# A rebuilt head and a rebuilt output norm in a hybrid decoder layer

## The chip, the cores and the metric

The kernel runs on one core of a Trainium2 chip. The metric is device time in microseconds (us) of one execution. The core has a TensorE (PE, with its weight loads as PEld), a VectorE (DVE), a ScalarE (ACT), a GpSimd (POOL) and a SyncE (SP), which here only issues DMAs.

## The reference, cut to what matters

One layer, one sequence of 512 tokens, width 2048, all in float32. The change touches the first norm with its modulation and the last norm.

```python
c_act = jax.nn.silu(c)
mod = c_act @ ada_w + ada_b                 # 2048 x 6144
shift, scale, gate = mod[:D], mod[D:2 * D], mod[2 * D:]
h = rms_norm(x, pre_gain) * (1.0 + scale) + shift
proj = h @ w_in                             # 2048 x 12416 columns
...                                         # RWKV-7 mixer, short convolution, their gates
m = sigmoid(g_a) * y_a + sigmoid(g_b) * y_b
o = m @ w_out
x = x + gate * rms_norm(o, post_gain)       # rms_norm(v, g) = v * rsqrt(mean(v*v) + 1e-6) * g
```

## The kernel before, in words

Everything up to the output product is transposed: channels lie on the 128 partitions, the 512 tokens along the free axis. x is 16 tiles `xT[k]` of 128 x 512, k over the channels. A product in float32 is made of three matmuls of rounded halves (`three`, lines 160 to 162): each operand is split into an upper half (`H`, by ACT) and the remainder (`L`, by POOL or DVE; `split`, lines 148 and 149).

The head (to line 297) has to bring the first tile of h to the PE. Its order is written out by hand for all five engines. SP issues 16 x tiles (line 202), with the two 1 MB pieces of `ada[0]` between the eighth and ninth x and behind the last; then three blocks of input weights (`fraw`, line 215), the two pieces of `ada[1]`, three more blocks, `ada[2]`, one block, `ada[3]`. `ada[j, 0]` holds the transposed columns of the shift for channels of tile j (128 x 2048), `ada[j, 1]` those of the scale. Their product with silu(c) is a reduction along the free axis on DVE (`columns`, line 245, with an accumulated sum); for that silu(c) lies as a row in all partitions in PSUM (`csr`, line 273, PE spreads a one-partition row `crow`). ACT then makes the two per-channel numbers `md` (`scales`, lines 251 and 252).

In the head the sum of squares over the channels is made by PE: ACT squares each x tile (line 268), PE adds them with a weight of ones into `pss` (line 270), turned per four tiles to another group of 32 columns. ACT copies the sums (line 275), PE brings the sums to tokens on partitions (`pst`, line 278), DVE makes the inverse root with integer start and three Newton steps (`rsqrt`, lines 139 to 144), spreads it (`rsb`, line 284), and PE turns it back to tokens along the free axis (`psr`, line 287). The pair `xs` (DVE, line 257), `hH` (ACT, line 259) and `hL` (DVE, line 262) gives the halves of the first h tile.

Behind it stands the joint: the first 16 output tiles of the input product (`fps`), begun while the other tiles of h are still being made, block after block of channels. Its order is computed by a planner in the kernel's text, which keeps a clock `now` and expected landings (`lands`, `come`) from constants, and writes out the order of all engines. Evictions of partial sums go to DVE (line 366) or to ACT and POOL (lines 370 and 371). From there to the end the order is likewise written out or given by Tile, and the PE's main work is `ps_c` (line 1041), the rest of the input product and the mixer beside it.

At the end the output product runs token-major: `o[i][n]` is 128 tokens by 512 columns, i over four rows of tokens, n over four quarters. The first three quarters keep `o` in SBUF, multiplied by `gg` (gate times post gain). For the last quarter the weights stay in SBUF and i is the outer loop: 48 matmuls, then ACT squares and sums (`osum`, line 1268), DVE multiplies by `gg` (line 1300) and makes the inverse root (lines 1301, 139 to 144), ACT and POOL make the first quarter of the output (lines 1303 and 1304), DVE the other three (line 1308), SP sends them (line 1309). For i = 3 nothing follows that could hide this.

Of the kernel before, what the change touches and what calls it, by code (L numbers as in the profile page):

```python
# [8 lines left out]
F32 = mybir.dt.float32  # L9
# [67 lines left out]
def trunk(ctx: ExitStack, tc: tile.TileContext, xT_d, x_d, prm_d, crow_d, ada1_d, ada2_d, rows_d, w_d, lora_d, pa_d, pb_d,  # L77
# [108 lines left out]
    with tc.tile_pool(name="ap", bufs=1) as ap, tc.tile_pool(name="psa", bufs=1, space=PSUM) as psa:  # L186
# [44 lines left out]
        orow = ap.tile([P, P], F32, name="orow")[0:1, :]  # L231
        G.memset(orow, 1.0)
# [3 lines left out]
        cth = ap.tile([P, D], F32, tag="ada", bufs=NADA, name="cth")[0:1, :]  # L236
        A.activation(cth, crow, AF.Tanh, scale=0.5)
        V.scalar_tensor_tensor(crow, cth, 1.0, crow, ALU.add, ALU.mult)
        csr = psa.tile([P, D], F32, name="csr")

        def columns(j, i):
# [3 lines left out]
            V.scalar_tensor_tensor(ada[j, i], ada[j, i], 0.5, csr, ALU.mult, ALU.mult, accum_out=accs[j][:, i:i + 1])  # L245
# [3 lines left out]
        def scales(j):  # L249
            md[j] = ap.tile([P, 2], F32, tag="md", bufs=3, name=f"md{j}")  # L250
            A.activation(md[j][:, 1:2], accs[j][:, 1:2], AF.Identity, bias=ab1[:, j:j + 1], scale=pc("pre", j))
            A.activation(md[j][:, 0:1], accs[j][:, 0:1], AF.Identity, bias=pc("ab", j))
# [12 lines left out]
        pss = bank("mm", "pss")  # L265
        for k in range(KT):
            sq = ap.tile([P, T], F32, tag="t", bufs=3, name=f"sq{k}")
            A.activation(sq, xT[k], AF.Square)
            g = 32 * (k % 4)
            TE.matmul(pss[g:g + 32, :], ones[:, 0:32], sq, start=(k < 4), stop=(k >= KT - 4), tile_position=(0, g))  # L270
# [4 lines left out]
        A.activation(sums, pss, AF.Copy)  # L275
        pst = bank("pg", "pst", 4)
# [1089 lines left out]
```

## Time and profile before

| | |
|---|---|
| median of the three runs shown | 1635.5 us |
| lowest and highest | 1628.7 and 1635.64 us |
| the profiled execution: time, span | 1627.16 us, 1625.1 us |
| its mean granted TensorE clock | 0.994 |
| busy: PE, weight load, DVE, ACT, POOL | 98%, 81%, 57%, 39%, 50% of the span |
| moved by DMA | 235.71 MB, mean 145 GB/s |

The numbers of the trace are from the one profiled execution and counted from its span's start. A row of the timeline has the start, the length, the engine (a q behind it for its queue), the line, the operation, what it writes and reads, and in brackets how long the engine had been idle and what ended that. Differences are to be set against 1627.16 us when they come from its rows, and against the median when runs are compared.

### The profile page before, as it was taken

Reading aid. Unit: us, or ns where it says so; the run is one execution under the profiler, and the core shown is the slowest. Engines: PE = TensorE matmul, PEld = TensorE weight load, DVE = VectorE, ACT = ScalarE, POOL = GpSimd, SP = SyncE. Lnnn points to the kernel's source line nnn. Section 1 sums busy time; section 2 is a strip of 40 time slices with the busy share of each in tenths; the row PEclk is TensorE's granted clock in tenths of the full one; section 3 lists DMA queues with packets and bytes.
Section 4 is the critical chain, followed back from the end, with each engine's and each line's share of the span. In section 5 each row is a group of like instructions: output and inputs, shape, how many; then the busy total and the mean of one; then the engine's idle time right before and its main releaser. Section 6 shows DMA issues by size and latency. Waiting matters only on the chain.

```text
span 1625.1 us, 23142 instructions
## 1 busy us (share of the span) xinstructions
PE 1593.1 (98%) x8152; PEld 1314.3 (81%) x8152; DVE 934.3 (57%) x1660; ACT 639.1 (39%) x1299; POOL 812.8 (50%) x649
## 2 busy tenths in 40 slices
PE   6999999999999999999999999999999999999997
PEld 2788878888888888888888888888888888888885
DVE  4998297863978827826869359353111354463315
ACT  4554352324545235335543353344433223322511
POOL 2699564553445534543535435434354446764421
PEclk8999999999999999999999999999999999999999
DMA  8986334333332342333333433433353886675704
GB/s 315 379 327 236 104 108 122 92 102 105 96 85 85 103 118 83 98 113 111 93 99 97 121 103 93 128 102 115 92 168 119 243 252 202 201 210 166 234 25 156
DMA packets 138885, 235.71 MB, mean 145 GB/s; under 512 B 34833, under 2 KB 43665, under 8 KB 134673
## 3 DMA queue, kind: packets, MB, share of 16 engines
q1 hardware_dynamic: 138624, 234.15, 46.3%
q8 instruction: 64, 1.05, 0.3%
q14 instruction: 51, 0.42, 0.1%
q10 hardware_dynamic: 146, 0.09, 0.0%
HBM read 214.79 MB, written 19.14 MB: 144 GB/s over the span
## 4 chain that ended last, share of the span: by engine, by line
PE 95%; DVE 3%; ACT 1%; issue 0%; DMA 0%; POOL 0%; DVEq 0%; ACTq 0%; POOLq 0%
PE ps_c L1041 53%; PE fps L162 3%; PE fps L161 3%; PE fps L160 3%; PE po L161 3%; PE po L160 3%; PE po L162 3%; PE py_a L162 2%; PE py_b L162 2%; PE py_a L160 2%; PE py_b L161 2%; PE py_b L160 2%; PE py_a L161 2%; PE pg L730 2%; PE pl L162 1%; PE pl L161 1%
## 5 line engine op out<-in xcount | busy, mean ns | idle before, releaser
L428 POOL TENSOR_TENSOR wL_c<-raw_c,wH_c 128x512 fp32r<-128x512 f32 x324 | 441.9, 1365 | 535.9 <-ACT wH_c L428 503.2
L1041 PE MATMUL ps_c<-hH,wL_c 128*128 128x512 f32 x1296 | 513.3, 396 | 0.7 <-POOL wL_c L428 0.7
L1041 PE MATMUL ps_c<-hH,wH_c 128*128 128x512 f32 x1296 | 513.6, 396 | 0.0
L1041 PE MATMUL ps_c<-hL,wH_c 128*128 128x512 f32 x1296 | 512.0, 395 | 0.0
L428 ACT ACTIVATE wH_c<-raw_c 128x512 fp32r<-128x512 f32 x324 | 204.1, 630 | 420.9 <-PE ps_c L1041 265.8
L1041 PEld LDWEIGHTS ps_c<-hH,wL_c 128*128 128x128 f32 x1296 | 243.7, 188 | 48.4 <-POOL wL_c L428 1.1
L1041 PEld LDWEIGHTS ps_c<-hL,wH_c 128*128 128x128 f32 x1296 | 243.8, 188 | 47.2
L1041 PEld LDWEIGHTS ps_c<-hH,wH_c 128*128 128x128 f32 x1296 | 243.8, 188 | 46.9
L149 POOL TENSOR_TENSOR fL<-fraw,fH 128x512 fp32r<-128x512 f32 x56 | 79.0, 1417 | 55.5 <-ACT fH L148 55.3
L428 DVE TENSOR_TENSOR invt<-M,Xg 128x60 f32<-128x60 f32 (+24 forms) x248 | 93.8, 378 | 7.9
L149 POOL TENSOR_TENSOR oL<-wo,oH 128x512 fp32r<-128x512 f32 x48 | 64.7, 1354 | 62.3 <-ACT oH L148 58.8
L160 PE MATMUL fps<-hH,fH 128*128 128x512 f32 x224 | 88.8, 396 | 3.6 <-ACT hH L259 3.6
L428 DVE TENSOR_TENSOR Xg<-Xg,invt 128x60 f32<-128x60 f32 (+24 forms) x248 | 87.2, 352 | 7.9
L161 PE MATMUL fps<-hL,fH 128*128 128x512 f32 x224 | 88.8, 396 | 1.9 <-DVE hL L262 1.9
L162 PE MATMUL fps<-hH,fL 128*128 128x512 f32 x224 | 88.4, 395 | 1.7 <-POOL fL L149 1.7
L428 DVE TENSOR_TENSOR GG<-pg,gmask 128x512 f32<-128x512 f32 x32 | 22.1, 692 | 108.5 <-PE pg L730 108.5
L245 DVE SCALAR_TENSOR_TENSOR ada<-ada,csr 128x2048 f32<-128x2048 f32 x32 | 72.6, 2277 | 10.0 <-PE csr L273 10.0
L161 PE MATMUL po<-oL,mH 128*128 128x512 f32 x192 | 74.9, 390 | 0.0
L160 PE MATMUL po<-oH,mH 128*128 128x512 f32 x192 | 74.7, 389 | 0.0
L162 PE MATMUL po<-oH,mL 128*128 128x512 f32 x192 | 74.7, 389 | 0.0
L148 ACT ACTIVATE oH<-wo 128x512 fp32r<-128x512 f32 x64 | 38.6, 627 | 74.9 <-PE po L162 49.6
L149 POOL TENSOR_TENSOR wL_pb<-raw_pb,wH_pb 128x512 fp32r<-128x512 f32 x32 | 42.5, 1330 | 45.3 <-ACT wH_pb L148 45.3
(268 smaller groups left out, 2584.4 us busy)
## 6 DMA issues: line engine op xcount, KB each, us to landing
raw_c<-in_w_dram SPq DMA_DIRECT2D x324, 256.0 KB, 2.7
ada<-in_ada_dram SPq DMA_DIRECT2D x32, 1024.0 KB, 9.3
gr<-in_ada_dram SPq DMA_DIRECT2D x64, 256.0 KB, 4.4
wo<-in_wo_dram SPq DMA_DIRECT2D x64, 256.0 KB, 3.9
fraw<-in_w_dram SPq DMA_DIRECT2D x56, 256.0 KB, 4.4
raw_pb<-in_pb_dram SPq DMA_DIRECT2D x32, 256.0 KB, 2.7
raw_pa<-in_pa_dram SPq DMA_DIRECT2D x32, 256.0 KB, 2.7
th_s<-th SPq DMA_DIRECT2D x30, 256.0 KB, 2.0
```

Source lines behind the costliest of these rows:

```text
L148: A.activation(H, src, AF.Copy)
L149: eng.tensor_tensor(L, src, H.bitcast(F32), ALU.subtract)
L160: TE.matmul(ps, wH, xH, start=start, stop=False)
L161: TE.matmul(ps, wH, xL, start=False, stop=False)
L162: TE.matmul(ps, wL, xH, start=False, stop=stop)
L245: V.scalar_tensor_tensor(ada[j, i], ada[j, i], 0.5, csr, ALU.mult, ALU.mult, accum_out=accs[j][:, i:i + 1])
L428: f(*args, **kw)
L730: TE.matmul(four(pg)[:, k, :], BK[:, c0 + k, i, :], AR[:, c0 + k, :], start=True, stop=True)
L1041: TE.matmul(ps, w[:, i, :], x[k], start=(k == k0 and x is hH and w is H), stop=(k == KT - 1 and w is L))
```

## The change

In the head, x comes first and without ada pieces between. Four DMAs of 512 KB bring `adan`, the shift's and scale's columns for tile 0 in the layout of the weights (channels of c on partitions). PE multiplies them with silu(c) (16 matmuls in four groups of 32 columns into `psc`, summed over the groups by a further matmul with `every`), so that DVE's two reductions of tile 0 go. ACT still squares x; DVE adds 13 of the squares to the first in SBUF (`acc`), PE sums this and the two left alone (8 and 12) over the channels at once into tokens on partitions. silu(c) as a row in all partitions now comes from `cs` by PE. The root is spread with a PE transpose. The planner's constants are set anew.

At the end the inverse root is a square root on ACT, a reciprocal on DVE and one Newton step. For i = 3 the second quarter is copied to PSUM by ACT, the third stays in PSUM and the fourth is multiplied in place in PSUM; DVE's order is written out for i = 3.

```diff
-        crow = ap.tile([P, D], F32, tag="ada", bufs=NADA, name="crow")[0:1, :]
-        A.dma_start(crow, crow_d)
...
         for k in range(KT):
             S.dma_start(xT[k], xT_d[k])
-            if k == 7:
-                fetch(0, (0,))
-        fetch(0, (1,))
+        adan = [ap.tile([P, KT // 2, 2 * P], F32, tag="ada", bufs=NADA, name=f"adan{i}") for i in range(2)]
+        for i in range(4):
+            q = slice(i % 2 * 4, i % 2 * 4 + 4)
+            S.dma_start(adan[i // 2][:, q, :], adan_d[i // 2, :, q, :])
...
-        orow = ap.tile([P, P], F32, name="orow")[0:1, :]
-        G.memset(orow, 1.0)
...
-        cth = ap.tile([P, D], F32, tag="ada", bufs=NADA, name="cth")[0:1, :]
-        A.activation(cth, crow, AF.Tanh, scale=0.5)
-        V.scalar_tensor_tensor(crow, cth, 1.0, crow, ALU.add, ALU.mult)
+        csb = ap.tile([P, KT, HB], F32, name="csb")
+        V.tensor_copy(csb, cs.unsqueeze(2).to_broadcast([P, KT, HB]))
+        every = ap.tile([P, 1], F32, name="every")
+        V.tensor_reduce(every, ident.rearrange("p (a b) -> p a b", b=HB)[:, :, 0], mybir.AxisListType.X, ALU.add)
+        pcs = bank("pg", "pcs")
+        TE.matmul(pcs[0:KT, 0:P], cs, ident, start=True, stop=True)
+        csT = ap.tile([P, P], F32, name="csT")
         csr = psa.tile([P, D], F32, name="csr")
+        def silu_rows():
+            A.activation(csT[0:KT, :], pcs[0:KT, 0:P], AF.Copy)
+            for k in range(KT):
+                TE.matmul(csr[:, k * P:(k + 1) * P], ident[0:KT, k:k + 1].to_broadcast([KT, P]), csT[0:KT, :], start=True,
+                          stop=True)
...
-        pss = bank("mm", "pss")
+        acc = ap.tile([P, T], F32, name="sqsum")
+        pst = bank("pg", "pst", 12)
+        def by_token(r, sq):
+            for i in range(4):
+                TE.matmul(pst[:, 4 * r + i:4 * r + i + 1], sq[:, i * P:(i + 1) * P], ones[:, 0:1], start=True, stop=True)
+        alone = (8, 12)
         for k in range(KT):
...
             A.activation(sq, xT[k], AF.Square)
-            g = 32 * (k % 4)
-            TE.matmul(pss[g:g + 32, :], ones[:, 0:32], sq, start=(k < 4), stop=(k >= KT - 4), tile_position=(0, g))
-            if k in (4, 6, 8, 10):
-                q = slice((k - 4) // 2 * T, (k - 2) // 2 * T)
-                TE.matmul(csr[:, q], orow, crow[:, q], start=True, stop=True)
-        sums = ap.tile([P, T], F32, tag="t", bufs=3, name="sums")
-        A.activation(sums, pss, AF.Copy)
-        pst = bank("pg", "pst", 4)
-        for i in range(4):
-            TE.matmul(pst[:, i:i + 1], sums[:, i * P:(i + 1) * P], ones[:, 0:1], start=True, stop=True)
-        columns(0, 0)
+            if k == 1:
+                silu_rows()
+            if k in alone:
+                by_token(1 + alone.index(k), sq)
+            elif k:
+                V.tensor_tensor(acc, acc, sq, ALU.add)
+        by_token(0, acc)
+        psc = bank("mm", "psc", 2 * P)
+        for k in range(KT):
+            g = 32 * (k % 4)
+            TE.matmul(psc[g:g + 32, :], csb[:, k, :], adan[k // 8][:, k % 8, :], start=(k < 4), stop=(k >= KT - 4),
+                      tile_position=(0, g))
+        sums = ap.tile([P, 2 * P], F32, name="sums")
+        A.activation(sums, psc, AF.Copy)
+        halve()
...
-            TE.matmul(psr[:, i * P:(i + 1) * P], rsb[:, i, :], ident, start=True, stop=True)
-        columns(0, 1)
-        halve()
-        scales(0)
+            TE.transpose(psr[:, i * P:(i + 1) * P], rsb[:, i, :], ident)
+        pcol = bank("pg", "pcol", 2)
+        for i in range(2):
+            TE.matmul(pcol[:, i:i + 1], sums[:, i * P:(i + 1) * P], every, start=True, stop=True)
+        scales(0, pcol)
...
-        clk = dict(dve=now + 1.4, act=now + 0.7, pool=now + 1.5, dma=now + 15.2)
-        ready, lands, cut = {0: now}, {1: now + 1.0, 2: now + 9.0, 3: now + 15.2}, {b: now + 0.4 * b for b in range(3)}
-        come = {b: now + 1.5 + 0.7 * (b - 3) for b in range(3, 6)}
-        come[6] = now + 9.7
+        clk = dict(dve=now + 1.4, act=now + 0.7, pool=now + 1.5, dma=now + 16.5)
+        ready, lands, cut = {0: now}, {1: now + 2.0, 2: now + 9.8, 3: now + 16.5}, {b: now + 0.4 * b for b in range(3)}
+        come = {b: now + 2.7 + 0.7 * (b - 3) for b in range(3, 6)}
+        come[6] = now + 10.5
...
-                o[i][n] = yslot(f"o{i}_{n}", pool=yc if n < 2 else yp)
+                o[i][n] = pso[i] if (i, n) == (3, NQ - 2) else yslot(f"o{i}_{n}", pool=yc if n < 2 else yp)
...
+            V.tensor_scalar(rs[:, 1:2], rs[:, 0:1], -0.5, None, ALU.mult)
...
+            if i == 3:
+                o1 = bank("pc", "o1")
+                A.activation(o1, o[i][1], AF.Copy)
+                o[i][1] = o1
...
             osum(i, NQ - 1, ps)
-            og = ev.tile([P, T], F32, tag=("u", "cv")[i % 2], bufs=1, name=f"ol{i}")
+            s3, r, y, u, h = ssq[:, i, NQ - 1:NQ], rs[:, 2:3], rs[:, 3:4], rs[:, 4:5], rs[:, 5:6]
+            A.activation(r, s3, AF.Sqrt, scale=1.0 / D, bias=rs[:, 0:1])
+            V.tensor_scalar(h, s3, -0.5 / D, rs[:, 1:2], ALU.mult, ALU.add)
+            og = ps if i == 3 else ev.tile([P, T], F32, tag=("u", "cv")[i % 2], bufs=1, name=f"ol{i}")
             V.tensor_tensor(og, ps, gg[NQ - 1], ALU.mult)
-            V.tensor_scalar(rs[:, 1:2], ssq[:, i, NQ - 1:NQ], rs[:, 0:1], 1.0 / D, ALU.add, ALU.mult)
-            rsqrt(rs[:, 2:3], rs[:, 1:2], rs[:, 3:4])
-            A.activation(o[i][0], o[i][0], AF.Copy, scale=rs[:, 2:3])
+            V.reciprocal(y, r)
+            V.scalar_tensor_tensor(u, y, h, y, ALU.mult, ALU.mult)
+            V.scalar_tensor_tensor(y, u, 1.5, y, ALU.add, ALU.mult)
+            A.activation(o[i][0], o[i][0], AF.Copy, scale=y)
```

More of the change, by code (lines that the diff above doesn't have):

```diff
@@ L244, in columns, with scales @@
                 accs[j] = ap.tile([P, 2], F32, tag="acc", bufs=3, name=f"acc{j}")
-            V.scalar_tensor_tensor(ada[j, i], ada[j, i], 0.5, csr, ALU.mult, ALU.mult, accum_out=accs[j][:, i:i + 1])
+            V.scalar_tensor_tensor(ada[j, i], ada[j, i], 1.0, csr, ALU.mult, ALU.mult, accum_out=accs[j][:, i:i + 1])
         xs, md = {}, {}
-        def scales(j):
+        def scales(j, sums=None):
+            sums = accs[j] if sums is None else sums
             md[j] = ap.tile([P, 2], F32, tag="md", bufs=3, name=f"md{j}")
-            A.activation(md[j][:, 1:2], accs[j][:, 1:2], AF.Identity, bias=ab1[:, j:j + 1], scale=pc("pre", j))
-            A.activation(md[j][:, 0:1], accs[j][:, 0:1], AF.Identity, bias=pc("ab", j))
+            A.activation(md[j][:, 1:2], sums[:, 1:2], AF.Identity, bias=ab1[:, j:j + 1], scale=pc("pre", j))
+            A.activation(md[j][:, 0:1], sums[:, 0:1], AF.Identity, bias=pc("ab", j))
         def modulate(j, rstd):
@@ new lines, in trunk @@
+        alone = (8, 12)
+        for k in range(KT):
+            if k == 0:
+                sq = acc
+            elif k in alone:
+                sq = ap.tile([P, T], F32, tag="s", bufs=3, name=f"sq{k}")
+            else:
+                sq = ap.tile([P, T], F32, tag="t", bufs=3, name=f"sq{k}")
+            A.activation(sq, xT[k], AF.Square)
+            if k == 1:
[4 more added lines that the diff above has]
+                V.tensor_tensor(acc, acc, sq, ALU.add)
@@ L280, in trunk @@
+        by_token(0, acc)
+        psc = bank("mm", "psc", 2 * P)
+        for k in range(KT):
+            g = 32 * (k % 4)
+            TE.matmul(psc[g:g + 32, :], csb[:, k, :], adan[k // 8][:, k % 8, :], start=(k < 4), stop=(k >= KT - 4),
[3 more added lines that the diff above has]
+        halve()
         ms = ap.tile([P, 3, 4], F32, name="ms")
[L281 removed]
+        V.tensor_reduce(ms[:, 0], pst.rearrange("p (r i) -> p i r", i=4), mybir.AxisListType.X, ALU.add)
@@ L282, in trunk @@
+        V.tensor_scalar(ms[:, 0], ms[:, 0], 1.0 / D, RMS_EPS, ALU.mult, ALU.add)
         rsqrt(ms[:, 1], ms[:, 0], ms[:, 2])
@@ L1288, in trunk @@
         for i in range(4):
-            rs = cst.tile([P, 4], F32, tag="rs", bufs=2, name=f"ors{i}")
+            rs = cst.tile([P, 6], F32, tag="rs", bufs=2, name=f"ors{i}")
             V.tensor_reduce(rs[:, 0:1], ssq[:, i, 0:NQ - 1], mybir.AxisListType.X, ALU.add)
-            V.tensor_scalar(rs[:, 0:1], rs[:, 0:1], D * RMS_EPS, None, ALU.add)
+            V.tensor_scalar(rs[:, 0:1], rs[:, 0:1], 1.0 / D, RMS_EPS, ALU.mult, ALU.add)
+            V.tensor_scalar(rs[:, 1:2], rs[:, 0:1], -0.5, None, ALU.mult)
             xr = [mslot(f"xr{i}_{n}") for n in range(NQ)]
@@ L1333, in _lay @@
                                                  lnx_bias, conv_w)], axis=1),
-        "crow": np.asarray(c).reshape(1, D),
+        "adan": np.concatenate([ada[:, 0:P], ada[:, D:D + P]], 1).reshape(2, KT // 2, P, 2 * P).transpose(0, 2, 1, 3),
         "ada1": ada[:, :2 * D].reshape(D, 2, KT, P).transpose(2, 1, 3, 0),
```

14 lines of the change are left out of this document (8 added, 6 removed).

## The prediction

> **What bounds the kernel now.** I read the page's head first, then the busy times by stretch, then the order of time in the first 31 us and the last 11, and last the DMA queue's waits. 0.5% of 1635.5 us, about the least that a measurement of this kernel can tell from no change, is 8.2 us.
>
> ```profile
> PE 95%; DVE 3%; ACT 1%; issue 0%; DMA 0%; POOL 0%; DVEq 0%; ACTq 0%; POOLq 0%
> 0.00:31.00 31.00, 17.60 (x57) 5.93 (x57) 12.05 (x29) 15.38 (x26) 4.54 (x18) 0.89 0.86 316
> 31.00:80.00 49.00, 43.93 (x174) 34.37 (x175) 42.33 (x44) 26.71 (x54) 28.18 (x22) 0.93 0.95 370
> 80.00:1614.00 1534.00, 1531.55 (x7924) 1274.04 (x7922) 874.30 (x1573) 595.57 (x1218) 778.42 (x610) 1.00 0.44 135
> 1614.00:1625.10 11.10, 0.00 (x0) 0.00 (x0) 5.63 (x16) 1.41 (x3) 1.68 (x1) 0.68 0.27 94
> ```
>
> The first line is the chain of work that ended last. The four after it are stretches: us, then busy PE, weight load, DVE, ACT and POOL, then granted clock, DMA share, GB/s. From 80 us to 1614 the PE is busy for 1531.55 of 1534 us: a us won ahead of that stretch reaches the end, and so does one won behind it. Three places can move: the head (31 us until the first product matmul), the joint behind it (31 to 80 us, 5.1 us of PE idle, DMA 0.95 busy) and the end (11.1 us without a matmul). The whole head and end are 42 us, 2.6% of the span.
>
> **The head.** In order of time (start, length):
>
> ```profile
> 14.14 1.05 PE L270 MATMUL pss<-sq,ones 128*32 128x512 f32 x4
> 22.22 1.05 PE L278 MATMUL pst<-ones,sums 128*128 128x1 f32 x8 [0.69 <-ACT sums L275]
> 23.31 0.16 DVE L281 TENSOR_SCALAR ms<-pst 128x4 f32<-128x4 f32 x1 [2.71 <-PE pst L278]
> 26.19 0.43 DVE L284 COPY rsb<-ms 128x512 f32<-128x512 f32 x1
> 26.53 2.28 DVE L245 SCALAR_TENSOR_TENSOR ada<-ada,csr 128x2048 f32<-128x2048 f32 x1
> 26.67 2.08 PE L287 MATMUL psr<-ident,rsb 128*128 128x128 f32 x8 [3.40 <-DVE rsb L284]
> 28.86 0.39 ACT L251 ACTIVATE md<-acc,ab,prm 128x1 f32<-128x1 f32 x1 [6.17 <-DVE ada L245]
> 29.27 0.75 DVE L257 SCALAR_TENSOR_TENSOR xs<-x,md,psr 128x512 f32<-128x512 f32 x1 [0.46 <-ACT md L251]
> 30.12 0.72 ACT L259 ACTIVATE hH<-xs,md 128x512 fp32r<-128x512 f32 x1 [0.17 <-DVE xs L257]
> 30.89 0.80 PE L160 MATMUL fps<-hH,fH 128*128 128x512 f32 x1 [2.14 <-ACT hH L259]
> ```
>
> Three steps stand one behind the other: the squares' sums (to 22.2, behind the last x tile), the root on DVE (23.31 to 26.19), and the second ada reduction behind it on DVE (26.53 to 28.8). The scale waits for the last. The change takes both 2.28 us reductions of tile 0 off DVE (two matmul groups take their place) and no longer feeds them through the same megabytes. When do the data land? The issue of the last megabyte of ada tile 0, its us from issue to landing, the pace in that stretch, and the squares as a group:
>
> ```profile
> 12.91 0.33 SPq L199 DMA_DIRECT2D ada<-in_ada_dram  x1
> ada<-in_ada_dram SPq DMA_DIRECT2D x1, 1024.0 KB, 7.3
> DMA packets 157, 0.29 MB, mean 410 GB/s; under 512 B 17, under 2 KB 17, under 8 KB 157
> L268 ACT ACTIVATE sq<-x 128x512 f32<-128x512 f32 x16 | 9.1, 619 | 5.4 <-PE pss L270 5.4
> ```
>
> Issued at 12.91, it lands at 20.2. At 410 GB/s its 1.05 MB take 2.56 us, an x tile 0.64. The last x tile is issued ahead of it, so it has landed at 17.6.
>
> - *x first.* SP issues 16 x tiles and then four adan pieces (512 KB each, 2 MB, as the two ada megabytes before). The last x lands at 17.6 less the other ada megabyte, which now stands between the eighth and the ninth x: 17.6 - 2.56 = 15.0. The last adan piece lands where the last ada did, 20.2. The crow load on ACT's queue goes; it lay beside the others.
> - *Squares by DVE.* ACT's 16 squares stay (0.62 us each, just below the arrival pace); they no longer wait for PE. 13 adds on DVE: no add of two SBUF operands stands in the head, the nearest row is 0.75 us (xs). So: last square 15.6, last add 16.4, four column sums (the x8 row of pst, 1.05) 17.5, reduce and scale 0.4, root 2.9 (23.31 to 26.19) less its 0.2: rsb at 20.6 to 21.1.
> - *Shift and scale by PE.* 16 matmuls of 32 columns by 256; the last four wait for the last adan piece. The pss row has two steps of 512 in 1.05, so 0.26 for one of 256. Ends: 0.5 (four column groups at once) and 1.8 (one after the other). I take four times 0.26, because that row has the same 32 columns: 21.25. Transposes: 2.08 if like psr now, half if they are one pass; I take 1.55: 22.8. Two column sums, half of the pst row: 0.53, so 23.35. The copy of the sums and the first weight split (ACT, 0.6 each) lie beside the transposes.
> - *From there as now*: scale 28.86 to 29.27, xs to 30.12, hH to 30.89: 2.03. First product matmul at 25.4. Ends: 24.7 (rsb at 21.1, one-pass transposes) and 26.7 (1.8 and 2.08). Against 30.9 that is 5.5, between 4.2 and 6.2.
> - *Hidden*: the 16 csr matmuls and the csT copy run while x lands (PE idles there); csb and every (DVE, each at most an rsb, 0.43) ahead of the first add. If that cover went, the csr matmuls would push the column sums, which have 3 us until psc ends. The removed tanh over crow and its product were hidden and bring nothing, nor does POOL's memset of orow. The ada buffers: crow and cth go, adan takes two, so the fetch of tile 2 finds free buffers; it still stands on SP's queue behind three weight loads that wait for the splits of POOL.
>
> **How much of it passes the joint.** SP's queue and the DMA engines in the 14 us around the start (40 slices of 0.35 us from 26), and two later issues:
>
> ```profile
> 17.07 14.62 SPq L215 DMA_DIRECT2D fraw<-in_w_dram  x3
> 31.74 0.93 SPq L199 DMA_DIRECT2D ada<-in_ada_dram  x2
> DMA  8899962100000000001599689999999889988669
> 39.98 0.97 SPq L199 DMA_DIRECT2D ada<-in_ada_dram  x2
> ada<-in_ada_dram SPq DMA_DIRECT2D x1, 1024.0 KB, 11.2
> 52.37 2.27 DVE L245 SCALAR_TENSOR_TENSOR ada<-ada,csr 128x2048 f32<-128x2048 f32 x1
> 59.40 2.28 DVE L245 SCALAR_TENSOR_TENSOR ada<-ada,csr 128x2048 f32<-128x2048 f32 x1
> 61.60 0.75 DVE L262 SCALAR_TENSOR_TENSOR hL<-xs,md,hH 128x512 fp32r<-128x512 f32 x1
> ```
>
> SP stands from 17.07 to 31.7 behind weight loads, and the engines run dry for about 12 slices, 4.2 us. With the splits 5.5 us earlier SP is free at about 26.2, before the engines run dry (28.4): the whole transfer stream behind it moves forward by those 4.2 us, not by 5.5. The slack of the readers takes the rest: the ada megabyte issued at 39.98 lands at 51.2 and is read at 52.37, 1.2 us later. So 4.2 + 1.2 = 5.4 us can pass. The order of the joint is planned anew with landings 0.8 to 1.3 us later after the start; what that does to 5.1 us of PE idle the trace does not show, and I bound it by one DVE reduction either way (2.2 us). I take 5.0 of the 5.5.
>
> **The end.**
>
> ```profile
> 1614.05 0.60 ACT L1268 ACTIVATE osq<-pl 128x512 f32<-128x512 f32 x1 [6.46 <-PE pl L162]
> 1614.77 0.69 DVE L1300 TENSOR_TENSOR ol<-pl,gg 128x512 f32<-128x512 f32 x1 [4.80 <-ACT osq L1268]
> 1615.38 0.20 DVE L1301 TENSOR_SCALAR ors<-ssq,ors 128x1 f32<-128x1 f32 x1
> 1617.74 1.42 DVE L1308 SCALAR_TENSOR_TENSOR xr<-o,ors,xr 128x512 f32<-128x512 f32 x2
> 1618.52 3.13 SPq L1309 DMA_DIRECT2D out_dram<-xr  x4
> 1618.60 1.68 POOL L1304 TENSOR_TENSOR xr<-o,xr 128x512 f32<-128x512 f32 x1 [9.17 <-ACT o L1303]
> 1619.08 1.75 DVE L1308 SCALAR_TENSOR_TENSOR xr<-ol,ors,xr 128x512 f32<-128x512 f32 x1
> 58.52 2.56 POOL L371 TENSOR_TENSOR firsts<-firsts,fs 128x512 f32<-128x512 f32 x2
> 58.79 0.69 DVE L366 TENSOR_TENSOR firsts<-fps,firsts 128x512 f32<-128x512 f32 x1 [0.67 <-PE fps L162]
> ```
>
> From 1615.38 to 1617.74 DVE makes the root: one step of 0.24 and 11 of 0.19. The new one: h (0.2) and the product by gg (0.61 to the next start) on DVE, the square root on ACT beside them, then reciprocal and two steps (3 x 0.19): y at 1614.77 + 0.24 + 0.61 + 0.58 = 1616.2, against 1617.74: 1.5 us. No row has a reciprocal; its ends are the 0.20 and the 0.69 of this fence, and I take 0.19 as for the other one-column steps. The last step on xr takes 1.75 now while POOL runs, 0.75 otherwise. Its operand comes from PSUM in the new kernel, and such a step took 0.69 in the middle of POOL work (last two rows): another 1.0. xr's three steps then end at 1618.2 instead of 1620.8. But y also starts ACT's product and POOL's add: 0.86 after y as now, and 1.28 without a neighbour (half of the two in 2.56), so 1618.4. SP sends the fourth output at 1618.7 and is done at 1619.1 instead of 1621.65: 2.55. The four then follow each other more closely than now, 1 MB in some 2 us, so I take 0.35 off for their own queue: the end gains 2.2 (1.9 to 2.6). In rows 0 to 2 the same edits hide behind the next row's 48 matmuls; the copy of o1 into PSUM (ACT, 0.6) falls into ACT's 6.5 us of idle time before its last square.
>
> **The sum.** 5.0 + 2.2 = 7.2 us. The profiled execution took 1627.16 us (span 1625.1): 1620.0. Its time is 8.3 below the median of the runs shown, which lie between 1628.7 and 1635.64; from the median it is 1628.3.
>
> **Rivals.**
>
> *The clock stays up* (18%). Now the first product matmuls run on half a clock (columns as above):
>
> ```profile
> 22.00:24.00 2.00, 1.05 (x8) 0.97 (x8) 0.65 (x2) 0.69 (x2) 1.17 (x1) 1.00 1.00 416
> 24.00:26.00 2.00, 0.00 (x0) 0.00 (x0) 1.65 (x11) 0.00 (x0) 0.09 (x1) 0.51 1.04 434
> 36.00:37.00 1.00, 1.00 (x4) 0.81 (x3) 0.26 (x2) 0.84 (x3) 0.09 (x1) 0.50 0.99 410
> ```
>
> The clock falls at 24 and is still 0.50 at 36. In the new head PE's pauses before the start are about 1.5 us instead of 3.4 and 2.1. At full clock psc and the transposes would end up to 1.3 us sooner, and the evictions that ACT does before the second scale too: 1.8 us more, 9.0 in all, 1626.5. Against it: PE's work there is thin (one-column and 32-column matmuls). The Trainium skill (TensorE: Matmul & The Clock Gate, Part 1) says that the clock follows activity in a window of about 3.4 us that runs freely; by that rule pauses of 1.5 us could leave it up. The trace agrees in so far as the clock fell after a stretch with little PE work.
>
> *The transfers hold the joint* (17%). The DMA engines are 0.95 busy there; if the stream moves only by its 4.2 us, and weight loads use up the readers' slack, the head passes 3 to 4 and the sum is about 5.5: 1630.
>
> *The square root costs the end its gain* (8%). One table load stands in the trace:
>
> ```profile
> 1.80 1.28 ACT L175 ACT_TABLE_LOAD   x1 [1.80 <-issue]
> ```
>
> If the root needs another table and each row's square takes the first one back, the last row has a 1.28 us load between its sum and its root: r at 1616.3, y at 1616.9, gain of the end 1.5 and of the whole 6.5: 1629. With one load in row 0 alone it is hidden, and that is what I expect. The Trainium skill (ScalarE: Activation LUTs, Table sets: the hidden batching unit) puts sqrt in a set of its own but cheap functions in every set, which makes it one load; with the drain that it adds (2.66 us, What ACT_TABLE_LOAD costs), a load in the last row would leave the end with almost nothing.
>
> *The new order of the joint stalls PE* (7%, the other side). DVE's order is written out: at 59.40 a reduction stands before the lower half hL (61.60) that PE waits for. If the new order puts two reductions (4.4 us) before such a step in two more places, PE loses 8.8: 1635.5 - 7.2 + 8.8 = 1637. At 7.2 us of new idle the gain is gone, at 15.4 the kernel is measurably slower. For it: DVE was busy for 42.33 of those 49 us. Against it: the landings move by 1.3 us at most.
>
> **Chances.** My forecast has 50%. Faster by over 0.5% needs 8.2 us: most of the clock's case, and a good third of the forecast's through its upper ends (6.2 and 2.6) and the spread of the runs: 0.38. Slower: part of the last rival, 0.05. Within: 0.57. The range takes in the lower runs (1628.7 - 9 = 1619.7) and the transfers' case from the highest (1635.6 - 3 = 1632.6), and leaves out the stalled joint.
>
> **What would show it.** First fps matmul at 24.7 to 26.7; no dry stretch of the DMA engines near the start; last x landed near 15; one second table load, near 1575; y about 1.5 us earlier after the last square; the last xr step 0.7 to 0.8; 8.9 us from the last matmul to the end. PE idle between start and 80 us over 7 us, or a start after 27, would make the prediction wrong.

## Result and profile after

The changed kernel takes 1620.38 us (median of five runs, 1618.96 to 1621.57) against 1635.5 us for the kernel before (five runs, 1628.7 to 1636.2): a ratio of 0.9914, 95% interval 0.9894 to 0.9935. The profiled execution took 1618.96 us (span 1617.0) against 1627.16 (span 1625.1), 8.2 us less. Of the 15.1 us between the medians only about 8 can be put down to the change: the times of the kernel before spread over 1626 to 1637 us, and four of its five runs here lie above 1635.

Stretches of the profile after (us, then busy PE, weight load, DVE, ACT, POOL, then granted clock, DMA share, GB/s):

```profile
0.00:31.00 31.00, 23.19 (x110) 18.65 (x111) 19.82 (x44) 16.23 (x29) 6.30 (x18) 0.90 0.97 359
31.00:80.00 49.00, 43.90 (x186) 34.59 (x185) 42.25 (x44) 28.61 (x57) 32.18 (x24) 0.99 0.95 368
80.00:1606.00 1526.00, 1523.61 (x7892) 1268.24 (x7891) 866.00 (x1548) 594.61 (x1216) 772.98 (x606) 1.00 0.45 135
1606.00:1617.00 11.00, 2.32 (x11) 1.59 (x9) 3.33 (x8) 1.70 (x4) 1.26 (x1) 0.79 0.29 95
```

PE's idle time between 31 and 80 us is 5.1 us as before (49 - 43.90), so the joint does not give the head's gain back as idle time. Timeline of the head, PE first and then the other engines around the start (start, length; one row joins the instructions of a line that follow without a pause):

```profile
6.08 7.19 PE L247 MATMUL csr<-csT,ident 16*128 16x128 f32 x32 [0.36 <-ACT csT L245]
13.21 3.57 PE L281 MATMUL pst<-ones,sq 128*128 128x1 f32 x16
16.64 1.85 PE L281 MATMUL pst<-ones,sqsum 128*128 128x1 f32 x8
18.42 3.51 PE L303 MATMUL psc<-adan,csb 128*32 128x256 f32 x32
21.86 0.66 PE L316 MATMUL psr<-ident,rsb 128*128 128x128 f32 x4
22.44 0.61 PE L319 MATMUL pcol<-every,sums 128*128 128x1 f32 x4
25.09 0.79 PE L160 MATMUL fps<-hH,fH 128*128 128x512 f32 x1 [2.04 <-ACT hH L269]
...
21.11 0.43 DVE L313 COPY rsb<-ms 128x512 f32<-128x512 f32 x1
23.09 0.35 ACT L261 ACTIVATE md<-pcol,ab,prm 128x1 f32<-128x1 f32 x1 [0.18 <-PE pcol L319]
28.35 2.29 DVE L254 SCALAR_TENSOR_TENSOR ada<-ada,csr 128x2048 f32<-128x2048 f32 x1
35.16 0.50 PE L160 MATMUL fps<-hH,fH 128*128 128x512 f32 x1 [1.48 <-ACT hH L269]
```

From 6.1 to 23.0 us PE has no pause: no bracket stands in its rows until the first product matmul. So PE's own work ended the head, not a landing: the last `adan` piece had landed at 19.86, the last x tile at 14.7. The first product matmul starts at 25.09 instead of 30.89, 5.80 earlier. The first matmul that needs the second h tile (tile 1) starts at 35.16 instead of 40.90, 5.74 earlier, and the last matmul of the kernel at 1607.93 instead of 1613.57, 5.64 earlier. These two in the kernel before:

```profile
40.90 0.49 PE L160 MATMUL fps<-hH,fH 128*128 128x512 f32 x1 [1.49 <-ACT hH L259]
1613.57 0.39 PE L162 MATMUL pl<-oH,mL 128*128 128x512 f32 x1
```

SP's queue, the DMA engines from 26 to 40 us (40 slices of 0.35 us), and the clock:

```profile
17.29 8.65 SPq L214 DMA_DIRECT2D fraw<-in_w_dram  x3
25.99 1.66 SPq L196 DMA_DIRECT2D ada<-in_ada_dram  x2
DMA  9999999999999989999979999999999999999879
25.00:26.00 1.00, 0.79 (x1) 0.28 (x1) 0.93 (x1) 0.56 (x2) 0.91 (x2) 0.54 0.96 398
28.00:30.00 2.00, 2.00 (x6) 1.59 (x5) 1.95 (x3) 0.63 (x3) 0.00 (x0) 0.50 1.10 408
```

SP is free at 25.99, and the 4.2 us in which the engines ran dry are gone. The clock falls at 25, as it fell before at 24.

The clock column needs care. In the trace the clock's record is a list of entries, each with a start, a length and a share; the column counts time that no entry covers as 1.00. The first entry of this profile stands at 21.67 us: 3.41 us at full clock, then 6.83 us at half from 25.09, then full from 31.91. In the profile before the first entry stands at 10.37: 13.65 us at full clock, then 13.65 us at half from 24.02. What the column shows ahead of a first entry is no measurement, and the pace of the matmuls says that the clock was at half there (shown with the head alone, below).

The end, in order of time:

```profile
1607.93 0.39 PE L162 MATMUL pl<-oH,mL 128*128 128x512 f32 x1
1609.08 0.29 ACT L1341 ACTIVATE ors<-ssq,ors 128x1 f32<-128x1 f32 x1
1609.81 0.15 DVE L1346 RECIPROCAL ors<-ors 128x1 f32<-128x1 f32 x1
1610.44 0.75 DVE L1353 SCALAR_TENSOR_TENSOR xr<-o,ors,xr 128x512 f32<-128x512 f32 x1
1611.22 2.14 SPq L1354 DMA_DIRECT2D out_dram<-xr  x4
1611.30 1.26 POOL L1350 TENSOR_TENSOR xr<-o,xr 128x512 f32<-128x512 f32 x1 [9.17 <-ACT o L1349]
1611.77 0.74 DVE L1353 SCALAR_TENSOR_TENSOR xr<-pl,ors,xr 128x512 f32<-128x512 f32 x1
```

The inverse root is ready 1.36 us after the sum (1609.08 to 1610.44) instead of 2.97 (1614.77 to 1617.74). The last step on `xr` takes 0.74 instead of 1.75 although POOL runs beside it. From the last matmul's end to the span's end it is 8.7 us instead of 11.1.

### The profile page after: what moved, and what is told of

The parts are those of the page before. It is cut to its first block, busy times and chain, and to the rows that moved or that the text cites. A ratio compares the mean times of both kernels' runs of the same rounds, so it can differ in the third digit from the quotient of the medians.

```text
span 1617.0 us, 23221 instructions
## 1 busy us (share of the span) xinstructions
PE 1593.0 (99%) x8194; PEld 1323.1 (82%) x8194; DVE 931.4 (58%) x1643; ACT 641.2 (40%) x1305; POOL 812.7 (50%) x648
## 3 DMA queue, kind: packets, MB, share of 16 engines
q8 instruction: 65, 1.06, 0.3%
## 4 chain that ended last, share of the span: by engine, by line
PE 95%; DVE 3%; ACT 1%; issue 0%; DMA 0%; POOL 0%; POOLq 0%; ACTq 0%
PE ps_c L1071 53%; PE fps L162 3%; PE fps L161 3%; PE fps L160 3%; PE po L161 3%; PE po L160 3%; PE po L162 3%; PE py_a L162 2%; PE py_b L161 2%; PE py_a L160 2%; PE py_b L160 2%; PE py_b L162 2%; PE py_a L161 2%; PE pg L760 2%; PE pl L162 1%; PE pl L161 1%
## 5 line engine op out<-in xcount | busy, mean ns | idle before, releaser
L149 POOL TENSOR_TENSOR fL<-fraw,fH 128x512 fp32r<-128x512 f32 x56 | 79.8, 1434 | 45.6 <-ACT fH L148 45.4
L458 DVE TENSOR_TENSOR Xg<-Xg,invt 128x60 f32<-128x60 f32 (+24 forms) x248 | 92.3, 372 | 7.9
L458 DVE TENSOR_TENSOR invt<-M,Xg 128x60 f32<-128x60 f32 (+24 forms) x248 | 87.1, 351 | 7.9
L254 DVE SCALAR_TENSOR_TENSOR ada<-ada,csr 128x2048 f32<-128x2048 f32 x30 | 68.1, 2275 | 0.0
```

Source lines behind the costliest of these rows:

```text
L149: eng.tensor_tensor(L, src, H.bitcast(F32), ALU.subtract)
L254: V.scalar_tensor_tensor(ada[j, i], ada[j, i], 1.0, csr, ALU.mult, ALU.mult, accum_out=accs[j][:, i:i + 1])
L458: f(*args, **kw)
```

## Experiments

**Head alone, end alone, and before again.** The first has the new head with the old end section, the second the old head with the new end; the third is the kernel before, unchanged, as a measure of what the comparison can tell.

```diff
 e1_head:  head, joint, planner constants of after; end section of before
 e2_end:   head, joint, planner constants of before; end section of after
```

> The new head alone, with the end of the kernel before. Theory (two independent gains): the first product matmul stands at 25.1 us as in the changed kernel, 5.7 us of that reach the last matmul, and the end keeps its 11.1 us: the span of the profile is 1619.4 us. Rival (the runs' larger difference of 15 us comes from the joint): the runs of this kernel alone already lie at 1621 to 1624, some 12 us below those of the kernel before, though the profile's span differs by 5.7.

> The new end alone, with the head of the kernel before. Theory: first product matmul at 30.9, last matmul as before, 8.7 instead of 11.1 us behind it: the profile's span is 2.4 us below that of the kernel before, 1622.7. Rival for the runs' 15 us: the end takes away something that the single profile of the kernel before did not show, and the runs fall by more than 5 us.

> The kernel before once more, to see in a profile where its runs of 1635 us lose 8 us against its profiled execution of 1627. Theory: the time differs from execution to execution in the joint or the head (PE idle between 0 and 80 us); a profile of about 1633 us span would show PE idle there above 5.1 us. Rival: the whole run is slower by the same share, as the pace of the matmuls from 80 us on would show (PE busy 1531.55 of 1534 us now).

Measured against the same 24 runs of the kernel before (median 1629.76): head alone 1623.68 (ratio 0.9946, 0.9926 to 0.9965), end alone 1626.76 (0.9981, 0.9961 to 1.0001), before again 1630.08 (1.0002, 0.9982 to 1.0023). 6.1 and 3.0 us: the parts add up to the whole (9.2 us for the changed kernel with the old planner constants, next experiment, against the same 24 runs). The interval of the end alone just reaches 1, so its gain is read from the profile: the last matmul starts at 1615.08 in a span of 1624.2, 9.1 us before the end against 11.5 (1613.57 to 1625.1), which makes 2.4 us.

Both profiles missed their expected spans, 1621.7 instead of 1619.4 (head alone) and 1624.2 instead of 1622.7 (end alone). The loss lies ahead of the last matmul: it starts at 1610.10 with the head alone, 2.2 us later than in the changed kernel, and with the end alone 1.5 us later than in the kernel before. What differs is the clock.

The kernel before does not run alike in all its executions, as its profile (first row) and that of its repeat show from 38 to 46 us:

```profile
38.00:46.00 8.00, 6.22 (x27) 4.60 (x26) 6.73 (x7) 3.50 (x8) 2.77 (x3) 1.00 0.92 350
...
38.00:46.00 8.00, 5.31 (x16) 3.70 (x15) 6.44 (x5) 3.69 (x8) 2.48 (x3) 0.79 0.98 386
```

In the repeat (second row) the clock falls a second time, to 0.79 on the mean, the trace has 16 matmuls instead of 27, and the span is 1.9 us longer (1627.0). The head alone had such a second stretch too (37.26 to 40.68 us), and its record of the clock begins late, with an entry at 30.44:

```profile
29.82 0.63 PE L162 MATMUL fps<-hH,fL 128*128 128x512 f32 x1
30.24 0.49 PE L160 MATMUL fps<-hH,fH 128*128 128x512 f32 x1
30.57 0.39 PE L161 MATMUL fps<-hL,fH 128*128 128x512 f32 x1
...
26.00:30.00 4.00, 3.82 (x9) 2.67 (x9) 4.00 (x4) 1.35 (x3) 1.57 (x2) 1.00 0.99 294
38.00:40.00 2.00, 2.00 (x6) 1.55 (x5) 2.00 (x3) 1.18 (x3) 1.29 (x1) 0.50 1.01 427
```

Up to this entry the matmuls are 0.43 us apart and last 0.63, in a stretch that the column puts at 1.00; behind it they are 0.23 apart and last 0.39, as at the end of the kernel. The same switch stands at the first entry of the other profiles (the squares in the kernel before last 1.06 us a pass ahead of 10.37 and 0.59 to 0.62 behind it). So PE ran at half its pace until the first entry, and in the changed kernel that is until 21.67.

**The planner's constants.** The changed kernel with the old constants of the joint's planner:

```diff
-         clk = dict(dve=now + 1.4, act=now + 0.7, pool=now + 1.5, dma=now + 16.5)
-         ready, lands, cut = {0: now}, {1: now + 2.0, 2: now + 9.8, 3: now + 16.5}, ...
+         clk = dict(dve=now + 1.4, act=now + 0.7, pool=now + 1.5, dma=now + 15.2)
+         ready, lands, cut = {0: now}, {1: now + 1.0, 2: now + 9.0, 3: now + 15.2}, ...
```

> The changed kernel with the planner's constants of the kernel before, so that the joint's order is written out as if the landings came 0.8 to 1.3 us earlier after the start. Theory (the new order only follows the start): within 1 us of the changed kernel, 1616 to 1618 us of span. Rival (the order is what carries the head's gain through the joint): PE idle between the start and 49 us later rises from 5 us to 7 or more, span 1619 or more.

1620.61 (1618.87 to 1622.69, ratio 0.9929, 0.9907 to 0.9951), span 1617.0: the same as the changed kernel, as expected. Between the orders that the planner writes out for the two sets of constants the runs show no difference. The second reduction of tile 1 waits 0.18 us for its megabyte there, and in the changed kernel it starts 0.02 us after the landing (28.33):

```profile
29.05 2.29 DVE L254 SCALAR_TENSOR_TENSOR ada<-ada,csr 128x2048 f32<-128x2048 f32 x1 [0.18 <-DMA ada<-in_ada_dram]
```

**The root alone at the end.** The changed kernel with its new root, but with the old operands: all four quarters from SBUF.

```diff
-    o[i][n] = pso[i] if (i, n) == (3, NQ - 2) else yslot(...)
+    o[i][n] = yslot(...)
...
-    o1 = bank("pc", "o1")
-    A.activation(o1, o[i][1], AF.Copy)
-    o[i][1] = o1
...
-    og = ps if i == 3 else ev.tile(...)
+    og = ev.tile(...)
```

> The changed kernel, but row 3's operands of the last step stay in SBUF as before; only the root is new. Theory: y still stands 1.36 us after the square's sum is read, but the last step on xr again runs beside POOL and takes 1.75 us instead of 0.74: 9.7 us from the last matmul to the end instead of 8.7 (11.1 in the kernel before). Rival (the root alone makes the gain, PSUM operands bring nothing): 8.7 us.

One run, 1622.74, span 1620.8; from the start of the last matmul (1610.79) to the end 10.0 us, where the changed kernel has 9.07 and the kernel before 11.5. So the root is worth 1.5 us and the operands in PSUM 0.9, as expected. The rest of its longer span lies ahead of the last matmul. The last `xr` step is slow again beside POOL:

```profile
1614.15 1.68 POOL L1346 TENSOR_TENSOR xr<-o,xr 128x512 f32<-128x512 f32 x1 [9.17 <-ACT o L1345]
1614.63 1.75 DVE L1349 SCALAR_TENSOR_TENSOR xr<-ol,ors,xr 128x512 f32<-128x512 f32 x1
```

**A table load in front of the root.** A tanh on one column ahead of each row's square and sum, so that the square root would have to load its table in every row:

```diff
+        dummy = cst.tile([P, 1], F32, tag="dummy", bufs=2, name="dummy")
+        A.activation(dummy, rs[:, 0:1], AF.Tanh)
         osum(i, NQ - 1, ps)
```

> The changed kernel with one tanh of a single column on ACT ahead of each last square, so that in every row, the last too, the square root's table is loaded anew between the square's sum and the root. Its result is not used. Theory: a load of 1.28 us stands on the path, y comes 0.8 to 0.9 us later (0.4 us of it is hidden beside DVE's product), end 9.6 us. Rival (the load also empties ACT's pipeline, 2.66 us by the Trainium skill, ScalarE: Activation LUTs, What ACT_TABLE_LOAD costs): y 2.2 us later, end 10.9 us.

One run, 1620.67, span 1618.6. The loads came in rows 0 to 2 only (three for the root, two for tanh) and none in row 3, so the case of the last row was not run. Row 2 shows the price:

```profile
1599.75 1.28 ACT L1343 ACT_TABLE_LOAD   x1
1601.05 0.29 ACT L1343 ACTIVATE ors<-ssq,ors 128x1 f32<-128x1 f32 x1
1602.02 1.42 DVE L1355 SCALAR_TENSOR_TENSOR xr<-o,ors,xr 128x512 f32<-128x512 f32 x2
```

The load starts 0.02 us after the sum is read (1599.73) and the root follows 0.02 us after it; the inverse root is ready 2.29 us after the sum (1602.02) instead of 1.39 (1609.05 to 1610.44 in the changed kernel): 0.9 later, as expected, though in row 2 and not in the last row. In the changed kernel the one extra load stands at 1576.5, in row 0, beside the 48 matmuls of the next row. The Trainium skill (ScalarE: Activation LUTs, What ACT_TABLE_LOAD costs) adds a drain of the pipeline to the load; the trace shows the load's 1.28 us and 0.02 us on either side of it, no drain.

**Shift and scale back on DVE.** The new head, but tile 0's two reductions as before:

```diff
-        for i in range(4):
-            S.dma_start(adan[i // 2][:, q, :], adan_d[i // 2, :, q, :])
+        fetch(0)
...
-        TE.matmul(psc[g:g + 32, :], csb[:, k, :], adan[k // 8][:, k % 8, :], ...)
-        A.activation(sums, psc, AF.Copy)
+        columns(0, 0)
...
-        TE.matmul(pcol[:, i:i + 1], sums[:, i * P:(i + 1) * P], every, ...)
-        scales(0, pcol)
+        columns(0, 1)
+        scales(0)
```

> The changed kernel with tile 0's shift and scale made by DVE's two reductions as before (both ada megabytes behind x); x first, squares by DVE and the new end stay. Theory (DVE's serial reductions are worth about 2 of the head's 5.8 us): reductions at 17.3 and 22.7, first product matmul at 27.0, span 1618.5 to 1619. Rival (the reductions are the whole gain): first product matmul at 29 or later, span above 1620.5. On the runs' spread: if it was PE's chain of squares that ran slowly in some executions of the old head, no run lies more than 4 us above the lowest; if it was DVE's reductions, some lie 7 us higher.

1622.98 (1620.97 to 1625.13, ten runs; ratio 0.9954, 0.9938 to 0.997), span 1620.1. The start moves to 27.73, 0.7 later than expected:

```profile
17.16 2.29 DVE L251 SCALAR_TENSOR_TENSOR ada<-ada,csr 128x2048 f32<-128x2048 f32 x1 [0.89 <-DMA ada<-in_ada_dram]
21.36 1.23 DVE L142 TENSOR_TENSOR ms<-ms 128x4 f32<-128x4 f32 x1
23.36 2.28 DVE L251 SCALAR_TENSOR_TENSOR ada<-ada,csr 128x2048 f32<-128x2048 f32 x1
27.73 0.80 PE L160 MATMUL fps<-hH,fH 128*128 128x512 f32 x1 [3.11 <-ACT hH L266]
```

So of the 5.8 us of the start, 2.6 (27.73 - 25.09) come from taking the reductions off DVE, and the other 3.2 (30.89 - 27.73) belong to the rest of the new head, x first and the squares by DVE above all. But in the root one step of 128 x 4 took 1.23 us, where its neighbours took 0.16; POOL was splitting a weight block from 21.31 to 22.57. This step lies on the path to the second reduction, so about 1.1 of the 2.6 us is this meeting of DVE and POOL (argued from the overlap, not tested), which the changed kernel avoids: there POOL starts at 23.05. None of the ten runs lies above 1625.13, though the reductions are back on DVE; so these alone are hardly what puts executions of the kernel before above 1632 us.

**A warm start.** The kernel before with eleven matmuls of the identity into an unused bank between 1.6 and 6.6 us, to see whether its runs above 1632 us come from a PE that begins on a low clock:

```diff
+        warm = bank("mm", "warm")
+        for _ in range(11):
+            TE.matmul(warm[:, 0:P], ident, ident, start=True, stop=True)
         pss = bank("mm", "pss")
```

> The kernel before with 11 small matmuls of ident on PE between 1.6 us and the first square; nothing reads them. In 19 of the 48 runs of kernels with the old head the time was above 1632 us, mostly at a mean clock of 0.988 to 0.990 instead of 0.993 to 0.994, which is some 16 us more on half a clock. Theory (those executions begin on a low clock and PE's chain of squares and csr, bound by PE, takes 8 us longer): with PE busy from the start no run is above 1630.5. Rival (the low clock comes from PE's pauses in the joint): about four in ten runs stay above 1632.

1627.59 (1625.51 to 1633.41, twelve runs; ratio 0.9993, 0.9978 to 1.0008). No gain, and two of the twelve still above 1632 us, at mean clocks of 0.989 and 0.988 (of the kernel before, measured beside it, seven of 21). The clock did come up sooner, at 7.63 instead of 10.37, but it fell sooner too, at 17.87. A low clock at the start is not the cause, or not all of it.

**Two executions of the kernel before**, in the hope of a profile of one above 1632 us:

> The kernel before once more, one look, for a profile of an execution above 1632 us. If it is one: theory (PE's pauses in the joint bring the clock down a second and third time) shows stretches at 0.50 between 38 and 80 us that the profile of 1627 us does not have, about 16 us of them; rival (the squares in the head run on half a clock) shows them between 0 and 24 us, and a first product matmul after 35 us.

> The kernel before once more, one look, again for a profile of an execution above 1632 us. The look before this one took 1626.81 us and shows nothing of it. Theories as there: PE's pauses in the joint bring the clock down again (stretches at 0.50 between 38 and 80 us, some 16 us of them), or the head's squares run on half a clock (0.50 between 0 and 24 us, first product matmul after 35 us).

1626.81 and 1628.77 us: neither was one. But the second has a second stretch at half clock (41.22 to 44.63), and its last matmul starts 1.6 us later than in the first profile.

**PE's order in the head.** The changed kernel with the sum of squares in one group (no tile left alone), issued among the `psc` matmuls, and `pcol` ahead of the transposes:

```diff
-        alone = (8, 12)
+        alone = ()
...
+            if k == 3:
+                by_token(0, acc)
...
+        # pcol's matmuls ahead of the transposes
```

> The changed kernel with another order on PE in the head: all 15 squares added by DVE (none summed alone), the first four of the 16 shift-and-scale matmuls ahead of the column sums, the sums of the columns ahead of the transposes. Theory (PE works without a pause from 6 to 22 us, and its order, not the last adan piece at 19.9, ends the head): PE loses 3.6 us of single sums, but waits for the last add; shift and scale end at 21.4 instead of 21.9, first product matmul 0.3 to 0.5 us sooner, at about 24.7 to 25.2. Rival (the root's chain on DVE ends the head): rsb moves by as much as the column sums do, later, and the start does not move or comes up to 0.4 us later.

1621.26 (1620.69 to 1622.03; ratio 0.9951, 0.9936 to 0.9966), span 1619.3, start 26.49:

```profile
17.72 1.87 PE L281 MATMUL pst<-ones,sqsum 128*128 128x1 f32 x8 [0.39 <-DVE sqsum L297]
22.00 0.43 DVE L313 COPY rsb<-ms 128x512 f32<-128x512 f32 x1
23.68 1.09 PE L319 MATMUL psr<-ident,rsb 128*128 128x128 f32 x4
26.49 0.79 PE L160 MATMUL fps<-hH,fH 128*128 128x512 f32 x1 [1.72 <-ACT hH L269]
```

PE now waits for DVE's last add (0.39), the column sums begin at 17.72 instead of 16.64, `rsb` comes at 22.00 instead of 21.11, and the root's chain ends the head. Less work for PE, but later: the start comes 1.4 us later, where 0.3 to 0.5 sooner was expected. In the changed kernel both chains, root and PE, end within half a us of each other (21.54 and 21.93).

**Keeping the clock up.** The changed kernel with four wide matmuls into an unused bank ahead of the scales:

```diff
+        warm = bank("mm", "warm")
+        for _ in range(4):
+            TE.matmul(warm, ident, csb.rearrange("p k c -> p (k c)"), start=True, stop=True)
         scales(0, pcol)
```

> The changed kernel with four matmuls of 512 columns on PE between the column sums (23.1 us) and the first product matmul (25.1); nothing reads them. Theory (the clock falls because PE does little between 22 and 25 us): the clock stays at 1.00, the first 13 product matmuls go at 0.23 us each instead of 0.43, ACT's evictions ahead of the second scale end some 2 us sooner, the first matmul with tile 1 stands at 33.6 instead of 35.2, and 1 to 1.5 us of that reach the end: span 1615.5 to 1616. Rival (the transfers hold the joint): the matmuls run faster, but tile 1 or tile 2 then waits for its ada pieces, and less than 0.4 us reaches the end. On the runs' spread: none.

1621.46 (1619.86 to 1623.74; ratio 0.9952, 0.9937 to 0.9967), span 1620.6:

```profile
21.97 1.12 PE L316 MATMUL psr<-ident,rsb 128*128 128x128 f32 x4
23.59 5.71 PE L322 MATMUL warm<-csb,ident 128*128 128x512 f32 x8
28.74 0.79 PE L160 MATMUL fps<-hH,fH 128*128 128x512 f32 x1
36.00 0.50 PE L160 MATMUL fps<-hH,fH 128*128 128x512 f32 x1 [1.89 <-ACT hH L269]
```

It was expected to end 1 to 1.5 us sooner, and did not. The clock was not up when the extra matmuls began: the first entry of the record stands at 27.69, the transposes took 1.12 us instead of 0.66, and the eight passes 5.71, which pushed the first product matmul to 28.74. From there the product matmuls ran at full pace (0.23 us apart from 29.37 on), and this made up for the late start: the first tile's 21 matmuls end at 34.1 us, in the changed kernel at 33.7. So a start that is 3.65 us later (28.74 - 25.09) moves the first matmul with tile 1 only by 0.84 (36.00 - 35.16), and in both PE waits there for `hH` (1.89 and 1.48 us). What sets the joint is when tile 1 is ready, and that hangs on its landing at 28.33 and the DVE and ACT steps after it. The medians of the runs differ by 1.1 us (1621.46 against 1620.38).

**Clock and joint in all profiles.** Start of the first product matmul and of the first one with tile 1, the first entry of the clock's record (full clock from there), entries at half clock that begin between the first matmul with tile 1 and the last matmul, and the start of the last matmul:

| profile | product | tile 1 | first entry | half clock behind | last matmul |
|---|---|---|---|---|---|
| before | 30.89 | 40.90 | 10.37 | none | 1613.57 |
| before again (1626.81 us) | 30.89 | 40.90 | 10.38 | none | 1613.20 |
| warm start | 31.57 | 41.57 | 7.63 | none | 1613.72 |
| before, repeat | 31.65 | 41.41 | 12.00 | 42.72 to 46.13 | 1615.41 |
| before again (1628.77 us) | 30.95 | 40.34 | 10.50 | 41.22 to 44.63 | 1615.19 |
| end alone | 31.62 | 41.38 | 11.97 | 42.69 to 46.10 | 1615.08 |
| changed kernel | 25.09 | 35.16 | 21.67 | none | 1607.93 |
| old constants | 25.66 | 35.72 | 22.54 | none | 1607.92 |
| shift and scale on DVE | 27.73 | 37.72 | 33.69 | none | 1611.09 |
| head alone | 25.69 | 35.12 | 30.44 | 37.26 to 40.68 | 1610.10 |
| other PE order | 26.49 | 35.38 | 30.26 | 37.09 to 40.50 | 1610.22 |
| extra matmuls | 28.74 | 36.00 | 27.69 | 37.93 to 41.35 | 1611.56 |
| root alone | 25.67 | 35.44 | 31.13 | 58.44 to 61.85 | 1610.79 |
| table loads | 25.66 | 35.43 | 31.15 | 58.45 to 61.87 | 1609.50 |

Half clock ahead of tile 1 should cost little, since PE waits for tile 1 in all of them (1.3 to 2.4 us). Behind it an entry of 3.41 us, in which PE does half its work, is worth 1.7 us by estimate. Profiles with such an entry have their last matmul 1.4 to 2.2 us later with the old head, and 1.6 us later or more with the new one. The head's gain is therefore taken between profiles that are alike in this: without a later entry 5.3 to 5.8 us (three profiles with the old head against the changed kernel and the old constants), with one 4.3 to 5.9 us (three with the old head against head alone, root alone and table loads). What makes the clock fall a second time in one execution and not in the next stays open.

## Why the prediction was right, point by point

- *x first.* The last x tile was put at 15.0 and landed at 14.7, the last `adan` piece at 20.2 and 19.86. Right.
- *The csr matmuls hidden.* Wrong. They take 7.19 us (32 passes of 0.22, ahead of the clock's first entry) and end at 13.3; from there on PE has a queue. The prediction gave them no length, and named what would happen without cover: that the column sums are pushed. They were: PE reaches the sums of the two tiles left alone only at 13.21 (3.57 us), those of the added ones at 16.64 (1.85) and `psc` at 18.42.
- *Column sums in 1.05 us.* Mis-sized: 1.85 for the same eight passes. A pass took 0.23 us instead of 0.13, and a weight load 0.23 (first row below, changed kernel) instead of 0.12 (second row, kernel before). The price came from a row at full clock. In the changed kernel PE was still at half (first entry at 21.67), and 0.22 is what such a load took in the kernel before at a granted clock of 0.50 (third row). The sums ended at 18.5 instead of 17.5, yet `rsb` came at 21.11, the upper of the two values given (20.6 to 21.1).

```profile
16.57 1.83 PEld L281 LDWEIGHTS pst<-ones,sqsum 128*128 128x128 f32 x8
22.22 0.97 PEld L278 LDWEIGHTS pst<-ones,sums 128*128 128x128 f32 x8 [1.59 <-ACT sums L275]
26.67 1.78 PEld L287 LDWEIGHTS psr<-ident,rsb 128*128 128x128 f32 x8 [3.48 <-DVE rsb L284]
```

- *psc ends when the last piece of `adan` lands, 21.25.* It ended at 21.9, because PE began it at 18.42 and needed 3.51. Wrong reason, 0.7 off.
- *Transposes 1.55.* One pass, and 0.66, below the lower end of 1.04 (half of 2.08): the 2.08 had been measured at half clock, and here the clock had just come up. In the runs where it had not, they took 1.09 to 1.12. `pcol` took 0.61 for 0.53. These 0.8 us made up for the two points above. So 25.4 against 25.09 is right partly by errors that cancel, and that the clock rose in time for the transposes is luck: with the same head it did not in three other profiles, whose start is 25.66 to 25.69.
- *5.0 of 5.5 us pass the joint, capped at 5.4 by the transfers.* 5.64 of 5.80 passed here, 4.3 to 5.9 between profiles that are alike in the clock. SP free at 25.99 (26.2 put down) and no dry slice: right. The cap was mis-sized. It held the whole stream to the 4.2 us of the dry stretch. That is what the megabytes of tiles 2 and 3 gained (the last of tile 2 landed at 35.42 instead of 39.44, of tile 3 at 41.23 instead of 45.68), but those of tile 4, which the prediction read for the slack, gained 5.8: issued at 35.91, landed at 45.4, against 39.98 and 51.2. The old stream had two more thin stretches (0.85 busy from 38 to 40 us, 0.78 from 44 to 46), and they filled up too (0.95 and 1.01). The joint's idle time stayed at 5.1 us, and the experiment with the old constants shows that the new plan had no part in that.

```profile
35.91 0.89 SPq L196 DMA_DIRECT2D ada<-in_ada_dram  x2
ada<-in_ada_dram SPq DMA_DIRECT2D x1, 1024.0 KB, 9.5
```

- *The end 2.2.* 2.4. The root 1.61 us earlier (1.5), the last `xr` step 0.74 (0.7 to 0.8), POOL's add 1.26 (1.28), the extra table load at 1576.5 (near 1575). The reduced run parts it into 1.5 for the root and 0.9 for the operands in PSUM, as worked out.
- *The sum.* 7.2 put down, 8.2 between the two profiled executions (5.64 + 2.46 and the rest outside the span), 9.2 with the old constants against 24 runs of the kernel before, 15.1 in the first comparison. The prediction held a change of under 0.5% for the likelier (0.57); it came out at 0.86%, with an interval that excludes 0.5%. The median 1620.38 lies 7.9 us below the 1628.3 put down and only 0.7 above the lower end of the range, 1619.7, which took the 9 us of the clock's case off the lowest run. That it lies inside is luck in part.

That step, from the sum to a median, is what failed most. The prediction saw that the profiled execution lay 8.3 us under the median and carried this difference over to the new kernel; the new kernel does not have it. Leaving the warm start out, kernels with the old head ran 88 times in all, 31 of them above 1632 us; kernels with the new head ran 42 times, none above 1625.13. Of the 31 the clock is on record for 27. In 22 of these its mean was 0.988 or 0.989, in the runs below 1632 us it was 0.990 to 0.995. A mean lower by 0.006 is about 10 us of lost clock in 1630, which fits the 7 us or so that these executions take longer; this is an estimate. The other five show 0.996 to 0.999, but the mean counts time ahead of a record's first entry as full clock, so it does not speak for or against. Against the 38 runs of the kernel before that lie below 1632 us (median 1627.93, three comparisons) the changed kernel gains 7.6 us, about the sum. What puts an execution above 1632 us, and what in the new head keeps it out, stays open: no profile of such an execution was to be had, and the warm start did not abolish them.

The rivals. *Clock stays up*: did not happen. It was not up to begin with, rose at 21.67 and fell at 25.09 after a pause of 2.04 us; PE worked without a pause from 6.08 on, and what came ahead of `psc` (18.42) did not raise it. The Trainium skill (TensorE: Matmul & The Clock Gate, Part 1) has the clock follow activity in a window of about 3.4 us. The trace agrees as far as lengths go: the entries of the record before the long one are of 3.41 us or multiples of it (6.83 here, 13.65 in the kernel before). How much thin matmuls count as activity no run here separates. *Transfers hold the joint*: not borne out, 4.3 to 5.9 us passed where it allowed 3 to 4. *A table load in the last row*: none there; by row 2 of the run with more loads its price would have been 0.9 us (0.7 put down). *The new order stalls PE*: not borne out, the idle time stayed at 5.1 us and the old constants took equal time.

## What to carry to other kernels

Where a long stretch is bound by one engine, a us won ahead of it or behind it is a us of the whole: find out where the front part's chain passes from engine to engine, and give each helper its duration before calling it hidden; here 7.2 us of helper matmuls became the head's bound. Before the price of a matmul is taken from a row, find out which clock PE had there and which it will have in the new place; the spacing of equal matmuls tells it where the column does not. Before a difference is set against a median, see whether the times of the old kernel lie in two groups: the new one need not inherit the upper one. A step whose neighbour slows it (1.75 us for 0.74) can be had at its own pace by taking one operand from PSUM.

## What the runs showed of the hardware

- A step on DVE with two operands in SBUF takes 1.75 us while POOL works in SBUF, and 0.74 with one operand in PSUM, in the same place (changed kernel with SBUF operands, changed kernel).
- The same kinds of small matmul came at two paces: one-column sums at 0.13 us a pass (before) and 0.23 (after), four transposes in 0.66 us (after) and in 1.09 to 1.12 (the runs with another PE order and with the extra matmuls). The slower pace stands ahead of the first entry of the clock's record in each of them, the faster one behind it at full clock.
- A transpose of 128 x 128 is one pass (four instructions for 512 columns), the product with `ident` that it replaced two (eight).
- The clock column can read 1.00 where PE runs at half its pace: with the head alone the wide matmuls are 0.43 us apart up to 30.2 us and 0.23 from 30.57 on, and the first entry stands at 30.44.
- A reciprocal of one column takes 0.15 us on DVE and a square root 0.29 on ACT; the scaling of the sum and the eleven steps of integer start and Newton took 2.36 (1615.38 to 1617.74).
